# Loading the token-major x two tiles earlier, and starting the second FFN with two blocks for three

## The chip, the cores and the metric

The kernel runs on one core of a Trainium2 chip. The metric is the device time of one execution, in microseconds (us): 1877.27 us is the median of 3 runs before the change, which lie between 1876.15 and 1878.51.

## The reference, cut to what matters

One decoder layer in float32 on 256 tokens of 2048 features. The two FFNs are 5632 wide and stand ahead of and behind a mixer with two kinds of attention.

```python
def rms_norm(x, g):
    y = x * rsqrt(mean(x * x, axis=-1, keepdims=True) + 1e-6)
    return y * g

def swiglu(x, w_gate, w_up, w_down):
    return (silu(x @ w_gate) * (x @ w_up)) @ w_down

x = x + 0.5 * swiglu(rms_norm(x, ffn1_norm), ffn1_w_gate, ffn1_w_up, ffn1_w_down)
h = rms_norm(x, mix_norm)
o_a, o_b = sparse_attention(h @ w_in), latent_attention(h @ w_in)
x = x + concat([rms_norm(o_a, out_norm_nsa), rms_norm(o_b, out_norm_mla)]) @ w_out
x = x + 0.5 * swiglu(rms_norm(x, ffn2_norm), ffn2_w_gate, ffn2_w_up, ffn2_w_down)
```

## The kernel before, in words

**Layout.** The state `xT` holds x with features on partitions: 16 chunks `c` of 128 features by 256 tokens. The input of a matmul stage is `h`: chunk by chunk xT times the norm's gain, as a rounded high part and the rest (`norm_chunk`). The norm's factor per token, `rb`, is not part of `h`; it is multiplied in when a result leaves its PSUM bank, so matmuls start before it is known, but no bank can be evicted before it.

**Weights.** All weights pass one list, `seq`, of tiles of up to 1 MB (128 partitions by 2048 columns), in the order of use. `load` requests the next tile through SP's DMA queue into one of 4 `raw` buffers, as soon as the buffer's former tile is split; what `along` holds for that tile's number is requested ahead of it. A tile is split in parts of up to 1024 columns: ScalarE (ACT) casts a part to `w_hi` (`ahead`), VectorE (DVE) subtracts to get `w_lo` (`finish`), into 4 buffers of each, so a part is cast when the part four ahead of it has been used up. A 128x128 slice of weights then takes one pair of matmuls, `mm2`: `w_hi` with 512 columns and `w_lo` with 256 (line 264).

**FFN.** 44 blocks of 128 of the 5632 inner features in 4 groups of 11. A block is a gate and an up product: 16 slices each, accumulated in two PSUM banks, evicted by `swish` with ACT's copies, DVE's additions (`ff_g`, `ff_u`), multiplications by `rb` and a tanh. There are 8 banks: 4 "acc", 2 "s", 2 "t". The first 3 blocks of a FFN (`BEGIN`) are done at once, chunk by chunk of `h`, so that they can begin when `h` is only begun: gate and up of 3 blocks take 6 banks, two "s" and four "acc", and 96 slices. Their weights come in 8 tiles of 768 KB, each with two chunks for all 6 products. From the fourth block on, each takes two "acc" banks by itself.

**The factor.** In the first FFN `squares` loads x once more with tokens on partitions (`xt`, four quarters of 512 KB, requested along with tiles 8 and 9 of weights, counted from 0); ACT squares and sums each half quarter (8 instructions), DVE reduces. In the second FFN GpSimd (POOL) has summed the squares of xT on the way, and `spread`, called when the first three blocks are done, begins with small matmuls with `ones`. Then, in both, `rsqrt` gives `rc` (4 small DVE and 10 small GpSimd instructions), two transposes on PE (line 279) spread it over partitions, and ACT's copy is `rb`. The mixer has three more such places.

**Order.** Engines run their queues in order; the program writes the queues by a planner, `go`. It keeps a clock for PE, ACT (`S`), DVE (`V`), GpSimd (`G`) and the DMA, with fixed prices, and at each step of PE's work emits first the subtractions and casts that are due, then one due step of a side task (`squares`, `spread`, `swish`, ...), and else the next piece of dense matmul work up to its `yield`. Its prices: 0.07 us and 0.00104 us per column for DVE, 0.155 us and 0.0021 us per column for GpSimd and 0.1 us until its result can be used, 0.09 us and 0.000833 us per column for ACT, 2400 columns per us for PE (half of that after a stretch with little work), 360,000 bytes per us for the DMA. Waits at run time are by semaphores, so a wrong price shifts order, not results.

Line 128 is the helper through which all ACT, DVE and GpSimd instructions go, line 369 the DMA request of `fetch`.

Of the kernel before, what the change touches and what calls it, by code (L numbers as in the profile page):

```python
# [14 lines left out]
P = 128  # L15
T = 256
D = 2048
C = D // P
# [5 lines left out]
BIG = -1e30  # L24
RAW, SPLIT = 4, 4

BEGIN = 3
BANKS = {"acc": 4, "s": 2, "t": 2}
NEVER = 1e9
TOKENS = "0g1c"  # L30
# [15 lines left out]
def _layout(inp):  # L46

    f = {k: np.asarray(v)[0] for k, v in inp.items()}
    o = {}
# [10 lines left out]
         cols(f["mla_q_norm"][:P], 1), cols(f["mla_k_norm"][:P], 1)], axis=1)  # L60
    o["rgain"] = np.stack([np.broadcast_to(f[n][P:], (P, 64)) for n in ("mla_q_norm", "mla_k_norm")], axis=1)
    for n in ("ffn1", "ffn2"):
        w = np.stack([f[f"{n}_w_gate"][:, :BEGIN * P], f[f"{n}_w_up"][:, :BEGIN * P]], axis=1)
        o[f"{n}_first"] = w.reshape(8, 2, P, 2, BEGIN, P).transpose(0, 2, 1, 4, 3, 5).reshape(8, P, 2 * 2 * BEGIN * P)
        for m in ("gate", "up"):
            w = f[f"{n}_w_{m}"]
            o[f"{n}_{m}"] = w.reshape(C, P, NF, P).transpose(2, 1, 0, 3).reshape(NF, P, C * P)
        w = f[f"{n}_w_down"]
        o[f"{n}_down"] = w.reshape(NCH, CH, P, C, P).transpose(0, 3, 2, 1, 4).reshape(NCH, C, P, CH * P)
    w = f["w_in"]  # L70
# [20 lines left out]
    i = np.arange(P)[:, None]  # L91
    j = np.arange(T)[None, :]
# [6 lines left out]
    n = np.arange(32)  # L99
# [52 lines left out]
class _Layer:  # L152
# [169 lines left out]
    def weights(self):  # L322
        a = self.a
        seq, together = [], {}
        H = C // 2 * P

        def ffn(n):
            for k in range(NCH):
                for i in range(CH):
                    if k == 0 and i < BEGIN:  # L330
                        if i == 0:
                            seq.extend((a[f"{n}_first"][r], [768, 768] if r or seq else [384, 384, 768]) for r in range(8))
                        continue
                    for m in ("gate", "up"):
                        seq.append((a[f"{n}_{m}"][k * CH + i], [H, H]))
                together[len(seq)] = 3
                for d in range(C):
                    seq.append((a[f"{n}_down"][k, d], [6 * P, 5 * P]))

        def rows(x, w):  # L340
            for i in range(4):
                seq.append((x[i], [2 * w, 2 * w]))

        ffn("ffn1")
        together[len(seq)] = together[len(seq) + 2] = 2
        rows(a["w_cmp"], 512)
        for x, y in (("w_sel", "w1k"), ("w_win", "w1v")):
            for n, c in enumerate(WEAVE):
                seq.append((a[x if c == "a" else y][WEAVE[:n].count(c)], [1024, 1024]))
        for m in TOKENS:  # L350
            rows(*{"c": (a["w_ckv"], 320), "g": (a["w_gcq"], 408), "0": (a["w_q"][0], 512), "1": (a["w_q"][1], 512)}[m])
        for m, i in MERGE:
            seq.append({"q": (a["w_uq"][i % 4], [768, 384]), "k": (a["w_ukv"][i % 4], [1024]),
                        "p": (a["w_out"][i // 8, i % 8], [1024, 1024])}[m])
        ffn("ffn2")
        self.seq = seq
        self.parts = [(r, sum(s[:i]), n, i + 1 == len(s)) for r, (_, s) in enumerate(seq) for i, n in enumerate(s)]
        at = 0
        while at < len(self.parts):
            n = 2 * together.get(self.parts[at][0], 0)  # L360
            p = self.parts[at:at + n]
            self.parts[at:at + n] = p[0::2] + p[1::2]
            at += max(n, 1)
        self.raw, self.done, self.before, self.half = {}, {}, {}, []
        self.n_load = self.n_split = self.n_used = 0
        self.along = {}
# [122 lines left out]
    def ffn(self, h, ssq, after, first):  # L489
        key, gain = ("f1", G_FFN1) if first else ("f2", G_FFN2)  # L490
# [23 lines left out]
        def pair(spare=False):  # L514
            p = self.bank("s" if spare else "acc")
            return p.rearrange("p (a t) -> p a t", a=2)
# [9 lines left out]
        def squares(ap):  # L526

            x = ap.tile([P, CH, 2, T], F32, name="xt", tag="act", bufs=2).rearrange("p a b t -> p (a b t)")[:, :2 * D]
            x = x.rearrange("p (q b n) -> p q b n", q=4, b=2)
            src = self.a["xt"].rearrange("p b (q n) -> p q b n", q=4)  # L530
            for q in range(4):
                self.along[8 + q // 2] = self.along.get(8 + q // 2, []) + [(x[:, q], src[:, q])]
            ss = self.sp.tile([P, 2, 4], F32, name="xss", tag="xss")
            yield lambda: 0.0 if 9 not in self.along else NEVER
            for q in range(4):
                for tb in range(2):
                    yield self.fresh(x[:, q])
                    self.S.activation(x[:, q, tb], x[:, q, tb], AF.Square, accum_out=ss[:, tb, q:q + 1])
            yield self.fresh(ss)
            s = self.sp.tile([P, 2], F32, name="xs", tag="xs")  # L540
            self.V.tensor_reduce(s, ss, axis=mybir.AxisListType.X, op=ALU.add)
            yield from self.spread(s, D, key)

        def dense(ap):
            if first:
                self.spawn(squares(ap))
                yield
            for k in range(NCH):
                act = ap.tile([P, CH, 2, T], F32R, name="act", tag="act", bufs=2)
                for i in range(CH):  # L550
                    if k == 0 and i < BEGIN:
                        if i:
                            continue
                        yield self.slot("acc", 4)
                        yield self.slot("s", 2)
                        p = [pair(b < 2) for b in range(2 * BEGIN)]
                        b = c = 0
                        while c < C:
                            yield self.at(("h", gain, c))
                            w = self.take(P)  # L560
                            for j in range(w[0].shape[1]):
                                self.mm2(p[b], [x[:, j] for x in w], h[:, c], c == 0, c == C - 1)
                                b += 1
                                if b == 2 * BEGIN:
                                    b, c = 0, c + 1
                                if j == 2 and w[0].shape[1] > 3:
                                    yield
                            self.n_used += 1
                            if c == C:
                                if not first:  # L570
                                    self.spawn(self.spread(ssq, D, key))
                                for b in range(BEGIN):
                                    self.spawn(swish(ap, p[2 * b:2 * b + 2], act, k, b))
                            yield
                        continue
                    yield self.slot("acc", 2)
                    p = [pair() for _ in range(2)]
                    for m in range(2):
                        for half in range(2):
                            w = self.take(P)  # L580
# [8 lines left out]
                acc = {}  # L589
                first3 = [(d, lo, n) for lo, n in ((0, 6), (6, 5)) for d in range(3)]  # L590
                for d, lo, n in first3 + [(d, lo, n) for d in range(3, C) for lo, n in ((0, 6), (6, 5))]:
# [3 lines left out]
                    w = self.take(P)  # L595
# [794 lines left out]
```

## Time and profile before

| | us |
|---|---|
| median of 3 runs | 1877.27 (1876.15 to 1878.51) |
| the profiled execution | 1876.71 |
| its span, first to last instruction | 1874.9 |
| PE busy (98%) | 1845.0 |
| DVE busy (68%) | 1274.3 |
| ACT busy (48%) | 900.0 |
| POOL busy (7%) | 129.1 |
| mean granted clock of PE | 0.994 of full speed |

The page puts 95% of the chain of work that ended last on PE. From its second part, in 40 slices of the span:

```profile
PE   8999999999999999999999998999999999999999
PEclk9999999999999999999999998999999999999999
DMA  9446653665466546675233345546654665465544
```

A digit is a share in tenths (9 is 90% or more): of time busy, of the full clock, of the DMA engines' time. The first FFN covers the first 16 slices, the mixer the next 8, the second FFN the rest. A timeline row gives start, duration, engine, line, operation and tiles; in brackets stands how long the engine was idle before it and what released it.

### The profile page before, as it was taken

Reading aid. Unit: us, or ns where it says so; the run is one execution under the profiler, and the core shown is the slowest. Engines: PE = TensorE matmul, PEld = TensorE weight load, DVE = VectorE, ACT = ScalarE, POOL = GpSimd, SP = SyncE. Lnnn points to the kernel's source line nnn. Section 1 sums busy time; section 2 is a strip of 40 time slices with the busy share of each in tenths; the row PEclk is TensorE's granted clock in tenths of the full one; section 3 lists DMA queues with packets and bytes.
Section 4 is the critical chain, followed back from the end, with each engine's and each line's share of the span. In section 5 each row is a group of like instructions: output and inputs, shape, how many; then the busy total and the mean of one; then the engine's idle time right before and its main releaser. Section 6 shows DMA issues by size and latency. Waiting matters only on the chain.

```text
span 1874.9 us, 27507 instructions
## 1 busy us (share of the span) xinstructions
PE 1845.0 (98%) x10645; PEld 1608.9 (86%) x10645; DVE 1274.3 (68%) x2234; ACT 900.0 (48%) x1395; POOL 129.1 (7%) x264
## 2 busy tenths in 40 slices
PE   8999999999999999999999998999999999999999
PEld 6888888888888888888878897888888888888888
DVE  5667666666666669766688785666666666666665
ACT  6544444444444545555565444444444444444543
POOL 0000000000000005201122160000000000000000
PEclk9999999999999999999999998999999999999999
DMA  9446653665466546675233345546654665465544
GB/s 343 155 149 200 216 197 131 209 222 182 143 215 205 196 141 203 234 268 193 89 120 137 136 140 175 180 153 210 202 194 152 214 199 183 154 211 196 190 164 141
DMA packets 59828, 344.12 MB, mean 184 GB/s; under 512 B 7089, under 2 KB 9649, under 8 KB 33073
## 3 DMA queue, kind: packets, MB, share of 16 engines
q1 hardware_dynamic: 59696, 342.36, 53.3%
q8 instruction: 84, 1.38, 0.3%
q14 instruction: 48, 0.39, 0.1%
HBM read 340.24 MB, written 2.10 MB: 183 GB/s over the span
## 4 chain that ended last, share of the span: by engine, by line
PE 95%; DVE 2%; POOL 1%; issue 1%; ACT 1%; DMA 0%; SPq 0%; POOLq 0%; DVEq 0%; ACTq 0%
PE ps_acc L264 89%; PE ps_s L264 3%; PE ps_t L264 1%; PE ps_t L279 1%; DVE w_lo L128 1%; POOL nw_t L128 1%; DVE junk L128 0%; DMA raw<-in_ffn_first 0%; ACT w_hi L128 0%; POOL nw_v L128 0%; SPq L369 0%; DVE h L128 0%; ACT p_e L128 0%; POOL rc L128 0%; DVE wait L128 0%
## 5 line engine op out<-in xcount | busy, mean ns | idle before, releaser
L128 DVE TENSOR_TENSOR w_lo<-raw,w_hi 128x1024 fp32r<-128x1024 f32 (+4 forms) x733 | 797.8, 1092 | 492.5 <-ACT w_hi L128 488.2
L128 ACT CAST w_hi<-raw 128x1024 fp32r<-128x1024 f32 (+4 forms) x733 | 683.6, 935 | 731.1 <-PE ps_acc L264 700.5
L264 PE MATMUL ps_acc<-h,w_hi 128*128 128x512 f32 x2816 | 992.0, 394 | 3.9 <-DVE ff_g L128 2.6
L264 PE MATMUL ps_acc<-h,w_lo 128*128 128x256 f32 x2816 | 787.6, 280 | 0.0
L264 PEld LDWEIGHTS ps_acc<-h,w_hi 128*128 128x128 f32 x2816 | 529.6, 188 | 131.5 <-issue 3.3
L264 PEld LDWEIGHTS ps_acc<-h,w_lo 128*128 128x128 f32 x2816 | 529.7, 188 | 0.2 <-DVE w_lo L128 0.2
L264 PE MATMUL ps_acc<-act,w_hi 128*128 128x512 f32 (+1 forms) x1430 | 494.8, 390 | 0.0
L264 PE MATMUL ps_acc<-act,w_lo 128*128 128x256 f32 x1408 | 398.2, 283 | 0.0
L264 PEld LDWEIGHTS ps_acc<-act,w_hi 128*128 128x128 f32 x1430 | 267.1, 188 | 60.3
L264 PEld LDWEIGHTS ps_acc<-act,w_lo 128*128 128x128 f32 x1408 | 264.7, 188 | 0.0
L264 PE MATMUL ps_acc<-w_hi,h 128*128 128x512 f32 (+2 forms) x384 | 120.1, 381 | 0.0
L128 DVE SCALAR_TENSOR_TENSOR xT<-ps_acc,xT 128x256 f32<-128x256 f32 x254 | 107.5, 423 | 15.8 <-PE ps_acc L264 5.3
L128 ACT ACTIVATE ff_t<-ff_g 128x256 f32<-128x256 f32 x88 | 36.8, 418 | 151.1 <-DVE ff_g L128 149.1
L264 PEld LDWEIGHTS ps_acc<-w_hi,h 128*128 128x128 f32 x384 | 71.3, 188 | 12.8 <-issue 1.9
L264 PE MATMUL ps_acc<-w_lo,h 128*128 128x512 f32 (+2 forms) x192 | 71.7, 373 | 0.0
L128 DVE SCALAR_TENSOR_TENSOR ff_g<-ff_t,ff_g 128x256 f32<-128x256 f32 x88 | 37.4, 425 | 17.8 <-ACT ff_t L128 17.8
L128 POOL TENSOR_TENSOR ssq<-xT 128x256 f32<-128x256 f32 x2 | 1.7, 833 | 661.8 <-DVE xT L128 661.8
L264 PE MATMUL ps_acc<-mha,w_hi 128*128 128x256 f32 x256 | 46.8, 284 | 0.3 <-DVE y L128 0.3
L264 PE MATMUL ps_acc<-mhb,w_hi 128*128 128x256 f32 x256 | 46.7, 286 | 0.0
L264 PEld LDWEIGHTS ps_acc<-w_lo,h 128*128 128x128 f32 x192 | 36.2, 189 | 5.7 <-issue 0.7
L128 DVE TENSOR_TENSOR ff_g<-ps_acc,ff_t 128x256 f32<-128x256 f32 x86 | 35.9, 418 | 7.6 <-ACT ff_t L128 7.6
L264 PEld LDWEIGHTS ps_acc<-mha,w_hi 128*128 128x128 f32 x256 | 39.1, 189 | 1.8 <-issue 1.0
(220 smaller groups left out, 1239.0 us busy)
## 6 DMA issues: line engine op xcount, KB each, us to landing
raw<-in_ffn_down SPq DMA_DIRECT2D x128, 704.0 KB, 4.1
raw<-in_ffn_gate SPq DMA_DIRECT2D x82, 1024.0 KB, 4.8
raw<-in_ffn_up SPq DMA_DIRECT2D x82, 1024.0 KB, 4.9
raw<-in_w_out SPq DMA_DIRECT2D x16, 1024.0 KB, 4.9
raw<-in_ffn_first SPq DMA_DIRECT2D x15, 768.0 KB, 4.5
raw<-in_w_q SPq DMA_DIRECT2D x8, 1024.0 KB, 4.9
raw<-in_w_cmp SPq DMA_DIRECT2D x4, 1024.0 KB, 5.1
raw<-in_w_sel SPq DMA_DIRECT2D x4, 1024.0 KB, 4.8
```

The costliest lines, as they stand in the source:

```text
L128: r = f(*args, **kw)
L264: self.nc.tensor.matmul(out, l, r, start=start, stop=stop)
L279: self.nc.tensor.transpose(out, src, self.ident if ident is None else ident)
```

## The change

`xt` is requested along with tiles 6 and 7 of weights for 8 and 9, and `squares` waits for tile 7's request, not tile 9's. The second FFN begins with two blocks, its first weights lie in 4 tiles of 1 MB for 8 of 768 KB, and the third block is done like those behind it. The wait for a chunk of `h` stands ahead of each chunk's first slice, now behind the `take` of its part; a part of more than three slices is left at its half only where no chunk ends there.

```diff
--- before.py
+++ after.py
@@ -24,7 +24,9 @@
 BIG = -1e30
 RAW, SPLIT = 4, 4
 
-BEGIN = 3
+BEGIN = {"ffn1": 3, "ffn2": 2}
+
+FIRST = {"ffn1": 8, "ffn2": 4}
 BANKS = {"acc": 4, "s": 2, "t": 2}
 NEVER = 1e9
 TOKENS = "0g1c"
@@ -60,8 +62,9 @@
          cols(f["mla_q_norm"][:P], 1), cols(f["mla_k_norm"][:P], 1)], axis=1)
     o["rgain"] = np.stack([np.broadcast_to(f[n][P:], (P, 64)) for n in ("mla_q_norm", "mla_k_norm")], axis=1)
     for n in ("ffn1", "ffn2"):
-        w = np.stack([f[f"{n}_w_gate"][:, :BEGIN * P], f[f"{n}_w_up"][:, :BEGIN * P]], axis=1)
-        o[f"{n}_first"] = w.reshape(8, 2, P, 2, BEGIN, P).transpose(0, 2, 1, 4, 3, 5).reshape(8, P, 2 * 2 * BEGIN * P)
+        b, r = BEGIN[n], FIRST[n]
+        w = np.stack([f[f"{n}_w_gate"][:, :b * P], f[f"{n}_w_up"][:, :b * P]], axis=1)
+        o[f"{n}_first"] = w.reshape(r, C // r, P, 2, b, P).transpose(0, 2, 1, 4, 3, 5).reshape(r, P, 2 * C // r * b * P)
         for m in ("gate", "up"):
             w = f[f"{n}_w_{m}"]
             o[f"{n}_{m}"] = w.reshape(C, P, NF, P).transpose(2, 1, 0, 3).reshape(NF, P, C * P)
@@ -327,9 +330,10 @@
         def ffn(n):
             for k in range(NCH):
                 for i in range(CH):
-                    if k == 0 and i < BEGIN:
+                    if k == 0 and i < BEGIN[n]:
                         if i == 0:
-                            seq.extend((a[f"{n}_first"][r], [768, 768] if r or seq else [384, 384, 768]) for r in range(8))
+                            w = C // FIRST[n] * BEGIN[n] * P
+                            seq.extend((a[f"{n}_first"][r], [w, w] if r or seq else [w // 2, w // 2, w]) for r in range(FIRST[n]))
                         continue
                     for m in ("gate", "up"):
                         seq.append((a[f"{n}_{m}"][k * CH + i], [H, H]))
@@ -529,9 +533,9 @@
             x = x.rearrange("p (q b n) -> p q b n", q=4, b=2)
             src = self.a["xt"].rearrange("p b (q n) -> p q b n", q=4)
             for q in range(4):
-                self.along[8 + q // 2] = self.along.get(8 + q // 2, []) + [(x[:, q], src[:, q])]
+                self.along[6 + q // 2] = self.along.get(6 + q // 2, []) + [(x[:, q], src[:, q])]
             ss = self.sp.tile([P, 2, 4], F32, name="xss", tag="xss")
-            yield lambda: 0.0 if 9 not in self.along else NEVER
+            yield lambda: 0.0 if 7 not in self.along else NEVER
             for q in range(4):
                 for tb in range(2):
                     yield self.fresh(x[:, q])
@@ -542,34 +546,37 @@
             yield from self.spread(s, D, key)
 
         def dense(ap):
+            begin = BEGIN["ffn1" if first else "ffn2"]
             if first:
                 self.spawn(squares(ap))
                 yield
             for k in range(NCH):
                 act = ap.tile([P, CH, 2, T], F32R, name="act", tag="act", bufs=2)
                 for i in range(CH):
-                    if k == 0 and i < BEGIN:
+                    if k == 0 and i < begin:
                         if i:
                             continue
-                        yield self.slot("acc", 4)
+                        yield self.slot("acc", 2 * begin - 2)
                         yield self.slot("s", 2)
-                        p = [pair(b < 2) for b in range(2 * BEGIN)]
+                        p = [pair(b < 2) for b in range(2 * begin)]
                         b = c = 0
                         while c < C:
-                            yield self.at(("h", gain, c))
                             w = self.take(P)
-                            for j in range(w[0].shape[1]):
+                            n = w[0].shape[1]
+                            for j in range(n):
+                                if b == 0:
+                                    yield self.at(("h", gain, c))
                                 self.mm2(p[b], [x[:, j] for x in w], h[:, c], c == 0, c == C - 1)
                                 b += 1
-                                if b == 2 * BEGIN:
+                                if b == 2 * begin:
                                     b, c = 0, c + 1
-                                if j == 2 and w[0].shape[1] > 3:
+                                if n > 3 and 2 * j + 2 == n and b:
                                     yield
                             self.n_used += 1
                             if c == C:
                                 if not first:
                                     self.spawn(self.spread(ssq, D, key))
-                                for b in range(BEGIN):
+                                for b in range(begin):
                                     self.spawn(swish(ap, p[2 * b:2 * b + 2], act, k, b))
                             yield
                         continue
```

## Rows read from the trace of the kernel before

**Rows 1.** The page's first part: busy us, share of the span, instructions.
```profile
PE 1845.0 (98%) x10645; PEld 1608.9 (86%) x10645; DVE 1274.3 (68%) x2234; ACT 900.0 (48%) x1395; POOL 129.1 (7%) x264
```

**Rows 2.** Timeline of PE, first FFN's start: start us, us, engine line op out<-in.
```profile
42.20 0.28 PE L264 MATMUL ps_acc<-h,w_lo 128*128 128x256 f32 x1
...
46.82 0.69 PE L279 MATMUL ps_t<-ident,rc 128*128 128x128 f32 x2 [4.34 <-POOL rc L128]
...
48.79 0.77 PE L264 MATMUL ps_acc<-h,w_hi 128*128 128x512 f32 x1 [1.29 <-DVE ff_g L128]
...
52.08 0.39 PE L264 MATMUL ps_acc<-h,w_hi 128*128 128x512 f32 x1
```

**Rows 3.** Timeline of ACT over the same stretch.
```profile
27.70 0.84 ACT L128 CAST w_hi<-raw 128x768 fp32r<-128x768 f32 x1 [0.86 <-PE ps_acc L264]
...
32.17 0.83 ACT L128 CAST w_hi<-raw 128x768 fp32r<-128x768 f32 x1
...
39.22 0.63 ACT L128 ACTIVATE xt<-xt 128x512 f32<-128x512 f32 x1
```

**Rows 4.** Timeline of DVE around the end of the first FFN's start.
```profile
43.47 1.24 DVE L128 TENSOR_TENSOR w_lo<-raw,w_hi 128x1024 fp32r<-128x1024 f32 x1 [0.38 <-ACT w_hi L128]
...
48.22 0.42 DVE L128 TENSOR_TENSOR ff_g<-ps_acc,ff_t 128x256 f32<-128x256 f32 x1 [3.51 <-ACT ff_t L128]
```

**Rows 5.** Timeline of PE, second FFN's start.
```profile
1120.14 0.40 PE L264 MATMUL ps_s<-h,w_hi 128*128 128x512 f32 x1
...
1123.37 0.49 PE L264 MATMUL ps_acc<-h,w_hi 128*128 128x512 f32 x1 [1.31 <-DVE y L128]
...
1155.33 0.50 PE L264 MATMUL ps_t<-ones,ssq 128*128 128x1 f32 x4
...
1160.37 0.69 PE L279 MATMUL ps_t<-ident,rc 128*128 128x128 f32 x2 [4.54 <-POOL rc L128]
...
1162.35 0.77 PE L264 MATMUL ps_acc<-h,w_hi 128*128 128x512 f32 x1 [1.29 <-DVE ff_g L128]
...
1168.21 0.39 PE L264 MATMUL ps_acc<-h,w_hi 128*128 128x512 f32 x1
```

**Rows 6.** Windows: stretch, us, busy PE PEld DVE ACT POOL, PEclk, DMA share, GB/s.
```profile
30.00:40.30 10.30, 10.30 (x61) 8.99 (x60) 6.12 (x8) 9.31 (x22) 0.00 (x0) 1.00 1.00 409
...
855.00:1077.00 222.00, 212.66 (x1278) 183.65 (x1277) 165.81 (x541) 122.16 (x278) 44.19 (x140) 0.99 0.38 131
...
1162.30:1168.20 5.90, 5.86 (x18) 5.01 (x19) 4.51 (x13) 2.49 (x6) 0.00 (x0) 0.50 0.00 0
```

**Rows 7.** Timeline of PE at the mixer's first and last norm.
```profile
761.95 0.61 PE L264 MATMUL ps_t<-ones,ssq 128*128 128x1 f32 x4 [0.85 <-POOL ssq L128]
...
767.42 0.38 PE L279 MATMUL ps_t<-ident,rc 128*128 128x128 f32 x2
...
1076.17 0.69 PE L279 MATMUL ps_t<-ident,rc 128*128 128x128 f32 x2 [2.33 <-POOL rc L128]
```

**Rows 8.** Timeline of SP's queue; its waits to 62 us (total, times, longest).
```profile
20.20 0.33 SPq L369 DMA_DIRECT2D raw<-in_ffn_first  x1
...
20.58 1.30 SPq L369 DMA_DIRECT2D xt<-in_xt  x2
...
23.29 0.34 SPq L369 DMA_DIRECT2D raw<-in_ffn_gate  x1
...
23.67 1.27 SPq L369 DMA_DIRECT2D xt<-in_xt  x2
...
SPq L369 <- DVE w_lo L128: 23.0, 9, 3.8
```

**Rows 9.** DMA: issues near 20.2 and 23.3 us, KB, us to landing; tile xt.
```profile
raw<-in_ffn_first SPq DMA_DIRECT2D x1, 768.0 KB, 7.0
...
raw<-in_ffn_gate SPq DMA_DIRECT2D x1, 1024.0 KB, 8.9
...
DMA to landing us min/median/max: 7.9/9.1/10.3
```

## The prediction

> **What bounds the kernel now.** The page's first part comes first: TensorE (PE) is busy for 1845.0 of 1874.9 us [rows 1]. So a change of load order or of block count can win only where PE stands idle or runs at half clock, and I looked for those places: waits of PE, then its timeline, then the chain of waits there.
>
> In the first FFN PE ends the three-block start at 42.48 (42.20 + 0.28), idles 4.34 us until the transposes of `rc`, and starts the next block only at 48.79 [rows 2]. All six accumulating banks are full, and no block can be evicted without the norm's factor `rb`. What ends last is the sum of squares of x: ACT's last square at 39.22, VectorE's (DVE) reduction, four DVE and ten GpSimd instructions until 46.82, then `rb`, `ff_t`, `ff_g` [rows 2 to 4]. PE then runs five weight slices (a 512- and a 256-column matmul each) in the 3.29 us to 52.08.
>
> The second FFN repeats this. Its start at 1120.14 is held 1.31 us by DVE's `y`, which frees the sixth bank; the last block matmul is followed at 1155.33 by the sum of squares, the transposes wait 4.54 us, and the next block starts at 1162.35 [rows 5]. Nine slices then take 5.86 us, at a granted clock of 0.50, the lower of its levels (1.2 of 2.4 GHz) [rows 5, 6]. At full clock a slice takes (1155.33 - 1120.14 - 1.31) / 96 = 0.353 us.
>
> **Second FFN, two blocks.** Two blocks take two "s" and two "acc" banks; two "acc" banks stay free. Four terms:
> - The start asks for two "acc" banks, those of the last projection but one, so `y` of the last projection is no longer waited for: 1.3 us. Those last banks are next wanted at the third block, 64 slices or 22.6 us on.
> - From 1155.33 to 1162.35 are 7.0 us. In the changed kernel the third block (32 slices, 11.3 us) runs there while `rb` is made. What PE still does itself is the sum (0.50) and two transposes (0.38 at full clock, as at 767.42) [rows 5, 7]: 0.9 us. Remaining gain 6.1.
> - PE's queue is in order, so the transposes can now stop the third block. From sum to ready `rc` took 1160.37 - 1155.33 = 5.0 us. The planner prices this chain at 3.5 us (four DVE steps, ten GpSimd steps of 0.16 plus 0.1) and a slice at 0.325, and may insert after every second slice: so after 12 slices, really 0.5 + 4.2 = 4.7 us. Wait 0.3. The rows bound it: none where the mixer's first norm did the same behind 14 slices (767.42 - 761.95, less 0.5, at 0.353), 2.33 at its last norm [rows 7]. I take 0.3, nearest to the first, which has the same operands around it.
> - Without the long idle time the half clock goes: 5.86 - 9 x 0.353 = 2.7 us.
>
> Sum: 1.3 + 6.1 - 0.3 + 2.7 = 9.8 us. The weights are the same 6 MB for three blocks; casts become 12 of 1024 columns for 16 of 768 and 4 of 1024, under PE throughout. DVE's subtractions grow by a third, to 1.24 us [rows 4], but four parts ahead of PE.
>
> **First FFN, x earlier.** SP's queue now holds, behind tile 5 of weights (counted from 0, so the eighth is tile 7): x chunk, xt, xt, tile 6, x chunk, xt, xt, tile 7, gate. No instruction is added, and the four xt issues (0.65 us each, 1.30 for two) fall where SP waits for a free buffer anyway, 23.0 us in nine waits for DVE up to 62 us [rows 8]. The first two are put ahead of tile 6, the others ahead of tile 7, which SP issued at 20.20 and now issues within some 0.1 us of that. DMA is full in this stretch (share 1.00 at 409 GB/s, [rows 6]), so bytes only change places. Tile 7 landed at 20.20 + 7.0 = 27.2, the gate tile at 23.29 + 8.9 = 32.2 [rows 8, 9]: 2 MB in 5.0 us. Tile 6 now has as many bytes ahead as tile 7 had and lands at 27.2, tile 7 at 32.2, the last xt 1.25 MB after tile 6, at 30.3. Before it was 24.3 + 10.3 = 34.6. So xt gains 4.3 us.
>
> Are the weights late? Tile 6's first cast ran at 27.70, PE-bound, tile 7's at 32.17 [rows 3]: 0.5 us to spare, and nothing. But a cast stands three parts (6.3 us of PE) ahead of its matmuls and cast and subtraction take at most 0.83 + 1.24 = 2.1, so PE has 4.2 us more. Cost 0; if that cover were gone, 2.5 us per MB.
>
> ACT did the last square 4.6 us after its data; with the same lag it is at 34.9, and the 7.6 us from there to the transposes [rows 2, 3] give `rc` at 42.5, as the block ends. The planner puts the transposes there. Next late is then not `rc`: at the block's end the planner issues a cast and its subtraction before the eviction, and DVE is in that subtraction until 43.47 + 1.24 = 44.7; `ff_g` and PE's start took 0.57 us (48.22 to 48.79) [rows 2, 4]. PE starts at 45.3 for 48.79: 3.5 us. An `rc` up to 0.8 us later costs nothing.
>
> After this the clock is unknown: idle time shrinks from 6.3 to some 2.5 us. Before, five slices lost 3.29 - 5 x 0.353 = 1.5 us. After the 2.33 us wait the transposes took 0.69 and not 0.38, so half clock [rows 7]; after 1.31 us PE went on at full speed. I take the nearer, half clock, and 0.3 us for the transposes that leave the path. Bounds: 0 to 1.8. First FFN: 3.8 us.
>
> The Trainium skill (DMA: Bandwidth & Descriptors, section "Two DMAs through the same engine are not ordered") says that descriptors of one queue start in order but nothing orders copies across the sixteen engines. The trace agrees as to order here (tile 7 at 27.2, first xt at 28.5), and its copies of xt spread from 7.9 to 10.3 us to landing. Held strictly in order, the sum is as above; if the quarters and the tile behind them shared the engines evenly, the last xt would land near tile 7's 32.2, `rc` would come at 44.4, the first FFN would win 2.4 and not 3.8 us, and the time would be 1865.1.
>
> **The sum.** 9.8 + 3.8 = 13.6 us. The profiled execution took 1876.71 us (span 1874.9), so 1863.1; the median of the runs stands 0.56 above it: 1863.7.
>
> **Rivals.**
> 1. The earlier transfer is hidden or given back: ACT, busy for 9.31 of 10.3 us from 30 us on [rows 6], delays the squares, or weights come late. For it: tile 7's cast has no margin, and squares share ACT with casts. Against: 4.2 us of cover at PE. Only the second FFN wins: 1867.5; with xt 2 us late, as it would be if it shared the engines with the tile behind it, 1865.1, inside the forecast's own range.
> 2. The wait moves into the third block: transposes queued too early, 2.33 us and a slow stretch of 1.5 as after the first FFN's wait. For it: the mixer's last norm [rows 7]; against: its first. 0.3 becomes 3.8: 1867.2.
> 3. The clock stays up after the first FFN's shorter gap: 1.5 more, 1862.2.
> 4. Slower. The planner replans everything behind 40 us from its own clock. In the mixer from 855 to 1077 us PE idles 9.3 us of 222 [rows 6], in waits set by this order. A new order that puts transposes ahead of their data costs some 3.8 us each time; with four more such places (15.2 us) the gain is gone, from five on it is slower: 1863.7 + 5 x 3.8 = 1882.7. For it: the last norm shows one such place. Against: prices and dependencies in the mixer are unchanged, only its start shifts.
> 5. The change is not what it says: x is requested early but the planner leaves the squares, and two blocks leave PE waiting as three did, for banks. Then nothing moves: 1877. Against: the "acc" tag has four banks and the start takes two.
>
> **How the numbers follow.** Forecast 0.55 (its own range 1860.5 to 1866.5), rival 1 0.15, rival 2 0.12, rival 3 0.10, rival 4 0.04, rival 5 0.04. About 0.2% (3.75 us) can be told from no change. Faster: the first four, 0.92; same 0.04; slower 0.04. Range: down to rival 3 with 2.5 us for order effects, 1859.5; up past rivals 1 and 2, 1869.5.
>
> **What would show it.** In the profile after: xt copies issued before 20 us and the last square near 35; the first wait for `rc` under 1 us and the next block at about 45.3; at the second FFN no 1.31 us wait behind `y`, the third block's matmuls between sum and transposes, a wait for `rc` under 1 us, and no stretch at clock 0.50 behind it. The prediction is wrong if PE waits for `w_hi` or `w_lo` between 25 and 42 us, if the third block stops for more than 2 us, or if PE's idle time in the mixer differs by more than 3 us.

## The result, and the profile after

The changed kernel takes 1864.02 us (median of 6 runs, 1862.15 to 1865.17) against 1877.19 us for the kernel before in the same session: a ratio of 0.9929, 95% interval 0.9916 to 0.9941. The forecast was 1863.7 us. The profiled execution took 1863.18 us.

The page, for [rows 1]: the span, then each engine's busy time, its share of the span and its instructions.

```profile
span 1861.4 us, 27485 instructions
PE 1842.0 (99%) x10645; PEld 1607.3 (86%) x10645; DVE 1273.6 (68%) x2230; ACT 898.5 (48%) x1391; POOL 132.2 (7%) x264
```

**First FFN.** TensorE's timeline, for [rows 2]. In the kernel after, line 131 is the engines' helper, 267 the matmul, 282 the transpose, 373 the DMA issue.

```profile
41.98 0.28 PE L267 MATMUL ps_acc<-h,w_lo 128*128 128x256 f32 x1
43.39 0.43 PE L282 MATMUL ps_t<-ident,rc 128*128 128x128 f32 x2 [1.13 <-POOL rc L131]
45.11 0.47 PE L267 MATMUL ps_acc<-h,w_hi 128*128 128x512 f32 x1 [1.29 <-DVE ff_g L131]
45.53 0.39 PE L267 MATMUL ps_acc<-h,w_hi 128*128 128x512 f32 x1
```

The start ends at 42.26, the transposes wait 1.13 us for 4.34 before, and the next block begins at 45.11 for 48.79. The slices behind it take 0.35 us: no half clock. SP's queue, ScalarE (ACT), VectorE and GpSimd in this stretch, for [rows 3, 4, 8]:

```profile
14.90 1.48 SPq L373 DMA_DIRECT2D xt<-in_xt  x2
18.56 1.21 SPq L373 DMA_DIRECT2D xt<-in_xt  x2
21.16 0.33 SPq L373 DMA_DIRECT2D raw<-in_ffn_first  x1
```
```profile
34.51 0.63 ACT L131 ACTIVATE xt<-xt 128x512 f32<-128x512 f32 x1
44.12 0.38 ACT L131 COPY ff_t<-ps_acc 128x256 f32<-128x256 f32 x1
```
```profile
39.06 1.23 DVE L131 TENSOR_TENSOR w_lo<-raw,w_hi 128x1024 fp32r<-128x1024 f32 x1 [0.39 <-ACT w_hi L131]
41.20 1.23 DVE L131 TENSOR_TENSOR w_lo<-raw,w_hi 128x1024 fp32r<-128x1024 f32 x1 [0.91 <-ACT w_hi L131]
43.25 1.23 DVE L131 TENSOR_TENSOR w_lo<-raw,w_hi 128x1024 fp32r<-128x1024 f32 x1 [0.83 <-ACT w_hi L131]
44.53 0.42 DVE L131 TENSOR_TENSOR ff_g<-ps_acc,ff_t 128x256 f32<-128x256 f32 x1
```
```profile
39.30 1.07 POOL L131 TENSOR_SCALAR nw_t<-nw_t 128x2 f32<-128x2 f32 x1
41.28 1.19 POOL L131 TENSOR_SCALAR nw_v<-nw_t 128x2 f32<-128x2 f32 x1
43.14 0.19 POOL L131 TENSOR_TENSOR rc<-rc,nw_v 128x2 f32<-128x2 f32 x1
```

Read three things here. The last square begins at 34.51 for 39.22. At the end of the gap two inputs of `ff_g` are ready almost together: the subtraction ahead of it in VectorE's queue ends at 44.48, and `ff_t` at 44.50. And of GpSimd's tiny instructions (0.19 us) two took 1.07 and 1.19: each began while a subtraction of VectorE ran (39.06 to 40.29, 41.20 to 42.43) and ended 0.04 to 0.08 us behind it (40.37, 42.47). The kernel before has one such instruction in each FFN, here the first FFN's, then the second's:

```profile
43.73 1.07 POOL L128 TENSOR_SCALAR nw_t<-nw_t 128x2 f32<-128x2 f32 x1
```
```profile
1156.58 1.18 POOL L128 TENSOR_TENSOR nw_t<-rc 128x2 f32<-128x2 f32 x1 [31.08 <-DVE rc L128]
```

**Second FFN**, for [rows 5]: TensorE, then GpSimd and VectorE in the same stretch.

```profile
1115.80 0.40 PE L267 MATMUL ps_s<-h,w_hi 128*128 128x512 f32 x1
1138.20 0.50 PE L267 MATMUL ps_t<-ones,ssq 128*128 128x1 f32 x4
1142.74 0.28 PE L267 MATMUL ps_acc<-h,w_lo 128*128 128x256 f32 x1
1144.26 0.43 PE L282 MATMUL ps_t<-ident,rc 128*128 128x128 f32 x2 [1.23 <-POOL rc L131]
```
```profile
1139.46 1.18 POOL L131 TENSOR_TENSOR nw_t<-rc 128x2 f32<-128x2 f32 x1 [17.08 <-DVE rc L131]
1142.69 1.24 POOL L131 TENSOR_SCALAR nw_v<-nw_v 128x2 f32<-128x2 f32 x1
1144.01 0.19 POOL L131 TENSOR_TENSOR rc<-rc,nw_v 128x2 f32<-128x2 f32 x1
```
```profile
1139.37 1.22 DVE L131 TENSOR_TENSOR w_lo<-raw,w_hi 128x1024 fp32r<-128x1024 f32 x1
1142.62 1.23 DVE L131 TENSOR_TENSOR w_lo<-raw,w_hi 128x1024 fp32r<-128x1024 f32 x1 [2.03 <-ACT w_hi L131]
```

No wait for `y` is left; twelve slices of the third block stand between the sum and the transposes, which wait 1.23 us for 4.54. From the sum to the transposes are 6.06 us, 5.04 before.

**By stage.** Three places split every span: the mixer's first matmul on `h`, the second FFN's first matmul, the end. Each row is one profiled execution (its total is not the median), and each edit is told below.

| kernel | to the mixer | mixer | second FFN | median us |
|---|---|---|---|---|
| before | 756.73 | 363.41 | 754.76 | 1877.27 |
| after | 751.59 | 364.21 | 745.60 | 1864.02 |
| a_only | 753.51 | 359.54 | 754.25 | 1869.2 |
| b_only | 757.92 | 359.42 | 745.46 | 1864.57 |
| xt_45 | 753.32 | 359.42 | 745.46 | 1861.06 |
| later_f2 | 751.83 | 363.47 | 744.00 | 1861.67 |
| later_both | 755.72 | 360.32 | 743.96 | 1859.1 |
| two_two | 755.97 | 359.63 | 745.80 | 1863.96 |
| chain_dve | 751.75 | 363.79 | 743.96 | 1862.22 |
| hold_only | 751.80 | 363.37 | 745.53 | 1864.37 |
| drain_first | 751.06 | 359.77 | 743.97 | 1857.17 |
| chain_all | 750.70 | 358.91 | 743.99 | 1855.03 |
| chain_45 | 750.44 | 357.38 | 743.98 | 1854.25 |
| chain_56 | 749.89 | 358.18 | 744.03 | 1854.28 |

The change won 5.14 us up to the mixer and 9.16 in the second FFN; the mixer was 0.80 longer in this trace. A stage of one trace is good to about a microsecond: b_only, whose first FFN is that of before, reached the mixer 1.2 us later than before did. later_both's trace is that of its slowest execution (1862.05 us; the others took 1858.19 to 1859.64).

### The profile page after: what moved, and what is told of

The parts are those of the page before. It is cut to its first block, busy times and chain, and to the rows that moved or that the text cites. A ratio compares the mean times of both kernels' runs of the same rounds, so it can differ in the third digit from the quotient of the medians.

```text
span 1861.4 us, 27485 instructions
## 1 busy us (share of the span) xinstructions
PE 1842.0 (99%) x10645; PEld 1607.3 (86%) x10645; DVE 1273.6 (68%) x2230; ACT 898.5 (48%) x1391; POOL 132.2 (7%) x264
## 4 chain that ended last, share of the span: by engine, by line
PE 95%; DVE 1%; POOL 1%; ACT 1%; issue 1%; DMA 0%; SPq 0%; POOLq 0%; DVEq 0%; ACTq 0%
PE ps_acc L267 90%; PE ps_s L267 3%; PE ps_t L267 1%; PE ps_t L282 1%; POOL nw_t L131 1%; DVE w_lo L131 1%; DMA raw<-in_ffn_first 0%; POOL nw_v L131 0%; DVE junk L131 0%; ACT w_hi L131 0%; SPq L373 0%; ACT p_e L131 0%; POOL rc L131 0%; ACT p_t L131 0%; ACT wait L131 0%
## 5 line engine op out<-in xcount | busy, mean ns | idle before, releaser
L131 DVE SCALAR_TENSOR_TENSOR h<-xT,par,h 128x256 fp32r<-128x256 f32 x48 | 31.4, 654 | 14.3 <-ACT h L131 14.1
L131 POOL TENSOR_TENSOR sqp<-xT 128x256 f32<-128x256 f32 x30 | 38.4, 1280 | 35.8 <-DVE xT L131 24.7
```

Of the source, the lines that this page charges most:

```text
L131: r = f(*args, **kw)
```

## The experiments

**Each part alone.** a_only is the kernel before with the copy of x along with tiles 6 and 7:

```diff
-                self.along[8 + q // 2] = self.along.get(8 + q // 2, []) + [(x[:, q], src[:, q])]
+                self.along[6 + q // 2] = self.along.get(6 + q // 2, []) + [(x[:, q], src[:, q])]
-            yield lambda: 0.0 if 9 not in self.along else NEVER
+            yield lambda: 0.0 if 7 not in self.along else NEVER
```

> Of the kernel before, with xt requested along with tiles 6 and 7 of weights alone; three blocks stay in both FFNs. Theory: the first FFN's gain is the earlier sum of squares by itself, so the block behind the start begins near 45.1 us (48.79 before) without half clock behind it, and the mixer's first matmul comes 5.1 us earlier (756.73 before, some 751.6); the second FFN keeps its waits of 1.3 and 4.5 us and its half clock. From that 1872.1 us. PE's queue in the mixer is not that of the kernel before: the last norm's transposes stand some seven groups of three matmuls later, so their wait of 2.33 us and the half clock behind it, together 3.4 us, should shrink too: 1868.7. Rival: the gain needs the changed place of the wait for h, then the block stays at 48.8 us and the time is 1877 less what the mixer gives.

Measured 1869.2 us, ratio 0.9955 (0.9941 to 0.9968). b_only is the changed kernel with these two lines as they were (8 and 9).

> Of the changed kernel, with xt requested along with tiles 8 and 9 again: two blocks in the second FFN alone. Theory: the first FFN is that of before (next block at 48.8 us, five slices at half clock), and the second FFN wins 9.3 us by itself. That makes 1867.9. The mixer's queue again has its last norm's transposes later, which should give 3.4 us more: 1864.5. Rival: the second FFN's gain depends on where the mixer ends and comes out below 8 us, then over 1866.

Measured 1864.57 us, ratio 0.9931 (0.9919 to 0.9944). The totals came as expected, yet the parts do not add up: 8.3 and 12.9 us below before's 1877.5 there, 21.2 together, where both at once bring 13.2. The table shows why. In a_only and b_only the mixer is 3.9 to 4.0 us shorter than before; in the changed kernel it is not. TensorE's queue in the mixer is the same, row by row, before and after; in both single parts the planner has written another, the same one in both: from about 970 us on some 260 of the mixer's 2157 matmuls stand elsewhere, and the transposes of the last norm (the second of the two output norms; some expectations call it the second norm) stand behind 14 groups of three matmuls and not 6. The rest is the parts' own: the second FFN at 754.25 without and 745.46 with two blocks, and in the first FFN a_only's transposes at once, b_only's after a wait of 4.34 us as before. First a_only, then b_only, and the mixer's last norm in a_only (third row) and in the changed kernel (last row):

```profile
43.06 0.43 PE L279 MATMUL ps_t<-ident,rc 128*128 128x128 f32 x2 [0.28 <-POOL rc L128]
45.48 0.47 PE L264 MATMUL ps_acc<-h,w_hi 128*128 128x512 f32 x1 [1.99 <-DVE ff_g L128]
...
1072.90 0.43 PE L279 MATMUL ps_t<-ident,rc 128*128 128x128 f32 x2 [0.92 <-POOL rc L128]
```
```profile
47.61 0.69 PE L282 MATMUL ps_t<-ident,rc 128*128 128x128 f32 x2 [4.34 <-POOL rc L131]
```
```profile
1071.91 0.69 PE L282 MATMUL ps_t<-ident,rc 128*128 128x128 f32 x2 [2.33 <-POOL rc L131]
```

**The transposes later.** later_f2 asks for the second FFN's transposes 2 us later by the planner's clock, which puts them behind 18 slices of the third block and not 12; later_both does so for the mixer's last norm as well (3 us: behind 16 groups of three matmuls and not 6).

```diff
+LATER = {"f2": 2.0}              # later_both: {"f2": 2.0, "o1": 3.0}
-        yield self.fresh(self.rc)
+        yield self.fresh(self.rc) + LATER.get(key, 0.0)
```

> The changed kernel, with the planner told that the second FFN's rc is ready 2.0 us later than its prices say, so that the transposes stand behind 18 slices of the third block and not 12. The queue ahead of them is the same. Theory: the 1.23 us for which the third block stops were lost to transposes queued too early, and go: 1862.8 for 1864.0, and the transposes' wait is 0 to 0.1 us. Rival: rc is what the next blocks wait for anyway, or the eviction is then late for the fourth block; then PE waits as long at another place and the time stays at 1864.0.

> The changed kernel with the transposes of 1/rms put later in TensorE's queue in two places: in the second FFN behind 18 slices of the third block and not 12 (as in later_f2), and in the mixer's second norm behind 16 triples and not 6. Theory: the 2.33 us that TensorE waits there, and the half clock behind it (the transposes took 0.69 and not 0.43), are the price of asking for 1/rms too early, and nothing else waits for it. Then the mixer is 3.5 to 4 us shorter, as in the three runs where another order had the transposes later by chance, and the second FFN is as in later_f2: 1861.7 - 3.7 = 1858.0 (1857 to 1859). Rival: what made those three mixers shorter was another part of their order, or the vector work behind the norm is now late in its turn: the wait of 2.33 goes and another takes its place further on, 1860.5 to 1862.

Measured 1861.67 us (0.9904 to 0.9931 of before) and 1859.1 us (0.9892 to 0.9919). Neither set of transposes waits any longer; first later_f2 in the second FFN, then later_both in the mixer:

```profile
1144.46 0.38 PE L283 MATMUL ps_t<-ident,rc 128*128 128x128 f32 x2
```
```profile
1076.22 0.38 PE L283 MATMUL ps_t<-ident,rc 128*128 128x128 f32 x2
```

The second FFN is 1.6 us shorter than in the changed kernel (744.0 for 745.6): more than the wait of 1.23, so nothing was late in its turn. The mixer went from 363.47 in later_f2, which has the old order there, to 360.32; in TensorE's queue of the mixer only these transposes moved, and 3.0 of the 3.15 us lie behind this norm's sum (49.09 us from there to the second FFN, now 46.06). later_both had forecast 3.5 to 4 and came out just above its range. So these transposes alone cost 3 us where they stood. They are not all of the single parts' 3.9 us: behind this norm's sum a_only wins 2.4 (46.74 for 49.14 before), and 1.4 more between the sums of the two output norms (90.84 for 92.24), where its order differs too. Which of those moves gave the 1.4 was not taken apart.

**x earlier still.** xt_45 is the changed kernel with the copy along with tiles 4 and 5 (`4 + q // 2`, `5 not in self.along`).

> The changed kernel, with xt requested along with tiles 4 and 5. The first FFN's transposes then stand six slices ahead of the start's end. Theory: in the changed kernel the gap of 42.26 to 45.11 us is held as much by the subtraction that DVE does until 44.48 as by rc, so rc some 4 us earlier moves the next block by at most 0.5 us (to no earlier than 44.6). Rival: rc alone holds it, then the next block begins at about 43.4, 1.7 us earlier. Second rival: tiles 4 and 5 now come 2.5 and 5 us later and PE waits for w_hi or w_lo ahead of 30 us, and the block begins later than 45.1. The mixer's queue has the last norm's transposes later, worth 3.4 us by the same reckoning: 1860.5 by the theory, 1859 by the first rival, over 1862 by the second.

Measured 1861.06 us (0.9899 to 0.9926 of before). The total looks like the theory, but for another reason: the mixer has a_only's order, and up to the mixer it is 1.7 us longer than the changed kernel. TensorE, then VectorE:

```profile
41.55 0.43 PE L282 MATMUL ps_t<-ident,rc 128*128 128x128 f32 x2 [0.58 <-POOL rc L131]
46.80 0.47 PE L267 MATMUL ps_acc<-h,w_hi 128*128 128x512 f32 x1 [2.70 <-DVE ff_g L131]
```
```profile
45.09 1.22 DVE L131 TENSOR_TENSOR w_lo<-raw,w_hi 128x1024 fp32r<-128x1024 f32 x1 [1.86 <-ACT w_hi L131]
46.23 0.42 DVE L131 TENSOR_TENSOR ff_g<-ps_acc,ff_t 128x256 f32<-128x256 f32 x1
```

1/rms is there early and the block still begins late, because VectorE holds one more subtraction ahead of `ff_g`, and that one waits for its cast. So 1/rms is not the only thing that the gap waits for.

**Two blocks in the first FFN as well.** two_two:

```diff
-BEGIN = {"ffn1": 3, "ffn2": 2}
+BEGIN = {"ffn1": 2, "ffn2": 2}
```

> The changed kernel with the first FFN beginning with two blocks as well (its eight first tiles are a third smaller; the copy of x still goes along with the seventh and eighth). The transposes of 1/rms then stand behind 13 slices of the third block. Theory: in the changed kernel TensorE has nothing to do from 42.26 to 45.11 us except the 0.43 us of the transposes; with a third block in its queue that idle 2.4 us is filled, as it was in the second FFN. Its queue in the mixer also differs from the changed kernel's: the second norm's transposes come later there, which in three runs (a_only, b_only, xt_45) made the mixer 3.9 to 4.0 us shorter than before, against 0.8 longer in the changed kernel. Sum 1864.0 - 2.4 - 4.0 = 1857.6 (1856.5 to 1858.5), the first matmul of the mixer at about 749.2. Rival 1, the early part cannot be fed at two blocks' pace (a slice of x is consumed every 1.4 us and not every 2.1, while x, its copy and the weights share the DMA queue and ScalarE): TensorE waits for h or w_lo between 10 and 40 us about as long as it saves, and only the mixer's 4.0 remains, 1860 or above. Rival 2, 1/rms itself is late at about 43 us whatever is queued: the wait moves in front of the transposes, 1 us saved of the 2.4, 1859.

Measured 1863.96 us (0.9918 to 0.9943 of before), no faster than the changed kernel although its mixer is 4.6 us shorter: the theory falls. Rival 1 holds, with a larger price than given, and rival 2 beside it: TensorE waits 5.3 us for `w_lo` and `w_hi` before 34 us and 2.09 for 1/rms, which comes at 42.2 (43.3 in the changed kernel). It is busy for 27.29 of the 34 us from 8 to 42, for 32.85 in the changed kernel; behind 42.28 it has no gap. First the changed kernel, then two_two: busy time by engine, granted clock, DMA share, GB/s.

```profile
8.00:42.00 34.00, 32.85 (x185) 28.11 (x185) 23.61 (x37) 25.11 (x48) 2.76 (x7) 1.00 0.99 389
```
```profile
8.00:42.00 34.00, 27.29 (x144) 21.92 (x144) 22.04 (x39) 24.38 (x50) 5.29 (x9) 1.00 0.97 364
```

The DMA engines are full in both. With three blocks each slice of x feeds half as much work again, while the second FFN's x lies in SBUF already; that this is what keeps TensorE fed here is argued and not tested.

**Two bounds at one point.** By the changed kernel's rows `ff_g` waits for two things that end 0.02 us apart. chain_dve takes away the one behind 1/rms: the last ten instructions of 1/rms go to VectorE, in the two FFNs alone (`chain` is passed there).

```diff
-    def rsqrt(self, y, x, tag, scale, add):
+    def rsqrt(self, y, x, tag, scale, add, chain=None):
-        V, G = self.V, self.G
+        V, G = self.V, chain or self.G
```

> The changed kernel with the last ten instructions of 1/rms (two columns of 128 values each) on VectorE and not on GpSimd, in the two FFNs alone; TensorE's queue is the same in the first FFN and the mixer, and in the second FFN the transposes stand two slices earlier. In the changed kernel's trace most of GpSimd's ten take 0.2 us, but those that begin just behind a w_lo subtraction of VectorE take 1.07 to 1.24 us and end within 0.1 us of it. Theory: GpSimd is held out while VectorE's subtraction of two SBUF tiles runs, and that is why 1/rms came 6.1 us behind the sum in the second FFN and not 5.0; on VectorE the ten take 0.1 to 0.2 us each, 1/rms comes about 2.5 us behind the sum, and the 1.23 us wait for it goes. In the first FFN it comes 2.5 us earlier too, but the next block still begins at about 45.1, because what it waits for last there is VectorE's ff_g, which stands behind a w_lo that ends at 44.48, not 1/rms. Sum 1864.0 - 1.2 = 1862.8 (1862 to 1863.5). Rival 1: 1/rms is what the first FFN's gap waits for too: another 1.1 us less, 1861.7. Rival 2: the ten instructions push VectorE's w_lo subtractions back by 2 us and TensorE waits for w_lo instead: 1864 or above.

hold_only takes away the other: from the start's last matmul to the first block's `ff_g`, no tile is split (`self.hold = first` as the start ends, `False` behind `ff_u`'s addition).

```diff
-        if self.n_split >= min(self.n_used + SPLIT, len(self.parts)):
+        if self.hold or self.n_split >= min(self.n_used + SPLIT, len(self.parts)):
```

> The changed kernel with one thing altered at the end of the first FFN's start: ScalarE and VectorE split no further tile of weights between the start's last matmul and the first block's ff_g additions (those tiles are split right behind them). In the changed kernel the next block begins at 45.11 us, behind ff_g at 44.53; two things are ready for ff_g at almost the same time, VectorE's w_lo that stands ahead of it (ends 44.48) and ff_t, which comes behind 1/rms (1/rms 43.33, rb 43.85, ff_t 44.12 + 0.37). chain_dve took away the second alone, and the block began no earlier (45.23). Theory: the two bounds coincide, and taking away the first alone brings nothing either: next block at 45.0 to 45.2, total as the changed kernel, 1864.0 (1863.2 to 1864.8; order of the mixer unchanged). Rival: w_lo alone is the bound, the block begins at about 44.3, 1863.1 or below; and if the tiles held back come too late, TensorE waits for w_hi or w_lo between 45 and 60 us and it is above 1864.8.

drain_first has both edits.

> Both together: chain_dve's ten instructions on VectorE in the two FFNs, and no tile of weights split ahead of the first block's ff_g in the first FFN. Theory of the two bounds: with 1/rms ready before the start's end (transposes at 42.4 without a wait, as in chain_dve) ff_t can be copied at about 42.9 and ff_g added at 43.3, and the next block begins at 43.6 to 43.9 and not at 45.2: 1.5 us less than chain_dve, 1860.7. Its order of the mixer differs again (the second norm's transposes six triples later than in the changed kernel), which by the four runs that had them later is worth 3 to 4 us: 1857.2 (1856.3 to 1858.3). Rival 1: the next block waits for something else at 45 (the tiles held back): 1858.7. Rival 2: in the mixer the later place brings nothing: 1860.7.

Measured 1862.22, 1864.37 and 1857.17 us (0.9906 to 0.9933, 0.9916 to 0.9943, 0.9876 to 0.9903 of before). TensorE at the first FFN's gap, in chain_dve, hold_only and drain_first:

```profile
42.25 0.28 PE L267 MATMUL ps_acc<-h,w_lo 128*128 128x256 f32 x1
42.37 0.38 PE L282 MATMUL ps_t<-ident,rc 128*128 128x128 f32 x2
45.23 0.47 PE L267 MATMUL ps_acc<-h,w_hi 128*128 128x512 f32 x1 [2.48 <-DVE ff_g L131]
```
```profile
43.65 0.43 PE L283 MATMUL ps_t<-ident,rc 128*128 128x128 f32 x2 [1.14 <-POOL rc L131]
45.28 0.50 PE L268 MATMUL ps_acc<-h,w_hi 128*128 128x512 f32 x1 [1.20 <-DVE ff_g L131]
```
```profile
42.83 0.28 PE L268 MATMUL ps_acc<-h,w_lo 128*128 128x256 f32 x1
42.95 0.38 PE L283 MATMUL ps_t<-ident,rc 128*128 128x128 f32 x2
44.52 0.51 PE L268 MATMUL ps_acc<-h,w_hi 128*128 128x512 f32 x1 [1.20 <-DVE ff_g L131]
```

From the end of the start's last matmul (the first rows; 42.52 in hold_only) to the next block: 2.85 us in the changed kernel, 2.70 with the first bound gone, 2.76 with the second gone, 1.41 with both gone. Either alone is worth 0.1 to 0.2 us here, both 1.4. Of what drain_first wins over chain_dve by the table, only 0.7 us lie up to the mixer, as its start ended 0.6 us later. The other 4.0 lie in the mixer, where the planner put the last norm's transposes 6 groups of three later and moved nothing else; its expectation had reckoned with 3 to 4. In the second FFN chain_dve's ten instructions take 0.16 to 0.17 us each, one every 0.2; its first and last:

```profile
1139.16 0.16 DVE L131 TENSOR_TENSOR nw_t<-rc 128x2 f32<-128x2 f32 x1
1140.95 0.16 DVE L131 TENSOR_TENSOR rc<-rc,nw_v 128x2 f32<-128x2 f32 x1
```

That is 1.95 us for the 4.74 of GpSimd (1139.46 to 1144.20). The transposes no longer wait, and the stage became shorter by the same 1.6 us as in later_f2.

**The best version.** chain_all adds VectorE's ten instructions in the mixer's three norms (its expectation speaks of two); chain_45 and chain_56 are chain_all with the copy of x along with tiles 4 and 5, and 5 and 6.

> drain_first with the ten instructions of 1/rms on VectorE in the two norms of the mixer as well. Theory: at the second norm 1/rms then comes about 2.5 us behind its sum and not 5 to 6, and what is left of TensorE's wait there (0.92 us in the runs that had the transposes at that place) goes: about 0.9 us less than drain_first, 1856.3 (1855.3 to 1857.5). Rival: VectorE is the busier engine in the mixer (1/rms in its queue stands behind its vector work and holds up what follows): as drain_first or slower, 1857.2 to 1859.

> chain_all with the copy of x along with the fifth and sixth tile of weights. In drain_first and chain_all 1/rms was ready about 1.3 us before the start's end and stood in the queue behind it; what was left of the gap, 1.6 us, is transposes, copies and ff_g one after the other. With the copy earlier the transposes stand 9 slices ahead of the start's end, and rb is ready before it. Theory: what is left of the gap is then the copy ff_t, ff_g and the hand-overs alone, about 0.9 us: 0.7 us less than chain_all, 1854.3 (1853.3 to 1855.5). Rival 1: a cast of 1.05 us stands between rb and ff_t on ScalarE in this order, ff_t comes behind it and the gap stays at 1.6 us or grows: 1855 to 1856. Rival 2: the copy now delays the tiles of weights behind it in SP's queue, TensorE waits for w_hi or w_lo before 40 us: 1856 or above.

> chain_all with the copy of x along with the sixth and seventh tile of weights: the transposes then stand three slices ahead of the start's end, rb is ready at about its end, and no cast stands between rb and ff_t. Theory: the gap is about 1.0 us and not 1.6, 0.6 us less than chain_all: 1854.4 (1853.4 to 1855.5); if the cast is what decides, this one is the faster of the two. Rival: 1/rms is not yet there three slices ahead of the end, TensorE waits in front of the transposes instead, 1855 or above.

Measured 1855.03, 1854.25 and 1854.28 us: 0.9878 (0.9865 to 0.9892), 0.9883 (0.9866 to 0.9899) and 0.9884 (0.9869 to 0.9898) of before. All three beat the changed kernel by some 9 us (none of their intervals reaches its 0.9916), chain_all by 0.3 us more than its range allowed; between them the times do not decide. In the traces the gap's last wait is 1.20, 0.56 and 0.33 us. chain_56 has neither the cast nor 1/rms late:

```profile
41.60 0.38 PE L283 MATMUL ps_t<-ident,rc 128*128 128x128 f32 x2
43.38 0.50 PE L268 MATMUL ps_acc<-h,w_hi 128*128 128x512 f32 x1 [0.33 <-DVE ff_g L131]
```

0.9 to 2.4 us of these gains lie in a shorter mixer (357.4 to 358.9 for drain_first's 359.8), whose order differs again; which of its places gave what was not taken apart.

## Why the prediction was right

The mechanism was right in both FFNs, but for one term of the second, and the total was 0.3 us off. That it came so close is luck: by the table the first FFN won 1.3 us more than forecast, the second 0.6 less, and the mixer, put at nothing, took 0.8.

- **Second FFN, 9.8 us forecast, 9.16 found** (8.5 to 9.3 over the table's pairs of three and two blocks with GpSimd's wait in it). The wait for `y`, the filled 6.1 us and the half clock went as forecast. The wait for `rc` in the third block was 1.23 us and not 0.3. The step that failed is "From sum to ready `rc` took 5.0 us", taken over unchanged. The third block gives VectorE one more subtraction to do while 1/rms is made, and GpSimd is held by it: two instructions of 1.2 us for one before. The prediction had weighed these subtractions only against TensorE's need of weights. later_f2 and chain_dve each removed this wait and won 1.6 us.
- **First FFN, next block at 45.3 forecast, 45.11 found.** The copies were issued from 14.90 and 18.56 on and landed in the order of the queue: tile 6 at 26.2, the last copy at 29.3, tile 7 at 31.2, each 1.0 us before its forecast. So the case of evenly shared engines, priced at 1865.1, did not come. The last square lagged 5.2 us behind its data and not 4.6 and came at 34.51 (34.9 forecast); the subtraction that bounds `ff_g` ended at 44.48 (44.7). `rc` was ready at 43.33 and not at 42.5: from the last square to the transposes it took 8.9 us for 7.6, and 1.0 of that is GpSimd's second long instruction, which the kernel before did not have. That was within the 0.8 us said to cost nothing, and chain_dve and hold_only show that it cost nothing only because the other bound ended at the same point.
- **First FFN, 0.3 us for the clock.** This was the unsure term and it fell on rival 3's side: the clock stayed up, and the stage won 5.14 us for 3.8. By the other traces (below) that was the likelier side, five of seven; a chance of 0.10 looks too low.
- **Tile 7 "within some 0.1 us" of 20.20** was wrong: SP issued it at 21.16. The gate tile came at 23.03 (23.29 before), and TensorE waited for no tile between 25 and 42 us, as forecast. The casts that 12 of 1024 columns replace are 16 of 768 alone, without the "4 of 1024" (ACT and VectorE each ran 4 instructions fewer); no term rests on them.
- **Rival 2** came true in part, a wait of 1.23 us for its 2.33, without the slow stretch. **Rival 4's mechanism** is real, its sign was not: new orders of the mixer came up in a_only, b_only, xt_45, two_two and drain_first, and each made it 3.6 to 4.0 us shorter than before. In the changed kernel the order did not change, so its mixer's 0.8 us are not from it; later_f2, chain_dve and hold_only with the same order took 363.4 to 363.8. They lie where the clock fell, ahead of the first output norm: from 960 to 970 us the granted clock was 0.66 in the changed kernel and 0.83 in later_f2, and the mixer up to that norm's sum took 222.96 us for 222.02.

## What to carry to other kernels

Compare single parts of a change stage by stage, not by their totals: where a planner orders the queues, any edit can move a distant instruction and win or lose as much as the edit itself. When a wait ends, look for what else becomes ready at the same moment; here two inputs of one addition were 0.02 us apart, and only removing both paid. A chain of tiny dependent instructions is best kept off an engine that another's long instructions lock out, above all where the change fills the idle time with just those long instructions.

## What the runs showed of the hardware

**GpSimd held by VectorE.** In the changed kernel's rows the four GpSimd instructions that began within a `w_lo` subtraction (39.30, 41.28, 1139.46, 1142.69) took 1.07 to 1.24 us where the others take 0.2, and ended 0.04 to 0.08 us behind the subtraction. Three more in the mixer began so (760.09, 889.62, 1070.58; 1.11 to 1.28 us), and no GpSimd instruction of this size that did was short. The Trainium skill (SBUF — State Buffer, section "SBUF: two separate sides") says that VectorE and GpSimd share a pair of ports under an exclusive lock, which a VectorE instruction with two SBUF inputs holds to its end against a GpSimd instruction that reads SBUF. The traces agree. In the second FFN the two held instructions took 2.0 us more than two free ones; the rest of what chain_dve gained in the chain (4.74 us to 1.95) is the step from one instruction to the next, some 0.28 us on GpSimd and 0.20 on VectorE.

**The clock after a gap of some 2.5 us is not fixed.** TensorE stood idle in the first FFN's gap, without the transposes, for 2.42 us in the changed kernel, 2.43 in later_f2, 2.34 in hold_only, 2.48 in chain_dve and 2.70 in xt_45's last wait, and the granted clock stayed at the upper level. After 2.27 us in a_only and 2.43 in later_both it fell to 0.50, in a_only from 46.6 to 50.1, in later_both from 46.4 to 52.3. later_f2 and later_both have the same queues on all four engines up to the mixer. At the mixer's last norm, where the changed kernel, before, later_f2, chain_dve and hold_only have the same queue and the same wait of 2.33 us, it fell in four of the five and not in hold_only (transposes of 0.43 us). The columns of these rows: stretch, its length, busy time of TensorE, granted clock, DMA share, GB/s; later_f2, then a_only, then later_both.

```profile
48.00:50.00 2.00, 2.00 (x14) 1.00 0.51 209
```
```profile
48.00:50.00 2.00, 2.00 (x8) 0.50 0.56 234
```
```profile
48.00:50.00 2.00, 2.00 (x8) 0.50 0.96 406
```

The Trainium skill (TensorE: Matmul & The Clock Gate, "Part 1: The HAM clock gate") says that the number of matmuls at the lower level varies from run to run of one kernel; here the fall itself differed between executions of the same queues. In a_only six slices at half clock took 3.65 us (46.61 to 50.26), and six of 0.35 us are 2.1: the fall cost 1.5 us, half of what the changed kernel's runs lie apart (1862.15 to 1865.17).
